# Moving GpSimd's two-input operations to VectorE in the mixers, norms and output projections of a two-layer hybrid kernel

## The chip, the cores and the metric

The kernel runs on one core of a Trainium2 chip. The metric is device time of one execution in microseconds (us); lower is better. The engines are named as in the profile: PE is TensorE (PEld its weight loads), DVE is VectorE, ACT is ScalarE, POOL is GpSimd, SP is SyncE, which issues nearly all DMAs.

## What is computed

Two layers act on 640 tokens (128 of a context pass, 512 of a denoising step) of 1024 channels. Each layer is a normalised four-way mixer followed by a convolutional FFN, both with residuals:

```python
h = rmsnorm(x, norm1_w) * (1 + sc1) + sh1
pa, pb, pc, pd = split(h @ w_in)            # SSD, retention, S5, RG-LRU
y = concat([ssd(pa), ret(pb), s5(pc), lru(pd)]) @ w_out
x = x + g1 * y
h = rmsnorm(x, norm2_w) * (1 + sc2) + sh2
g, u = split(h @ w_up)
x = x + g2 * ((silu(dwconv(g)) * u) @ w_down)
```

The six vectors sh, sc, g come from a modulation matrix product of the conditioning vector. After the second layer there is one more rmsnorm. The final states of the four scans are outputs too.

## The kernel before

**Layout and precision.** Activations are held channels by tokens: eight tiles of 128 x 640, worked in two halves of 320 columns. The second half (`HALF[1]`) is done first everywhere (`HO = (1, 0)`). The first half holds the 128 context tokens and 192 of the others, which have different modulation, so a scaled operation needs two instructions there (128 and 192 columns, `CSEG`) and one of 320 in the second half.

**Three products for one.** A float32 product is made of three fp32r products (`mm3`): every operand is split into `hi` (rounded) and `lo = x - hi`. For weights this is done in `wsplit` (line 186): a DMA brings 128 x 512 floats into a ring of five `raw` buffers, ACT casts `hi`, and a TENSOR_TENSOR subtracts to make `lo`, after which the `raw` buffer is free. `lo` reads two SBUF operands. Which engine makes it alternates by a list:

```python
lo_eng = [G, V]
...
(le or lo_eng[lo_i[0] % len(lo_eng)]).tensor_tensor(lo, raw, hi, op=subtract)
```

`G` is GpSimd, `V` is VectorE. The first two weight tiles of a projection (`first_tiles`, line 232) ask for `G` by `le`.

**The norm** (`Norm`, line 358). `add` squares each of the eight tiles on ACT (`nsq`) and sums them (`nacc`), the sum alternating between G and V; a matmul with ones sums over channels; `rsqrt_of` makes `nrs` on DVE. `apply` then does for each k: `nt = x * am * nrs` (DVE), `hhi = nt + sh` (ACT), and `hlo`: for even k one DVE SCALAR_TENSOR_TENSOR per segment, for odd k `nt + sh` on ACT and then one subtraction on G.

**The mixers.** `s5_mixer` runs eight blocks, each a chain of matmul, four DVE operations, two scans (`s5r`), and the turn back, in which G makes two of four operations. `lru_mixer` ends in a product `ylru` on G. `ssd_mixer` works in five chunks for two head pairs; in each, `sE` goes ACT, DVE, ACT, G, DVE. `ret_mixer` rotates four tiles (`rq`, one product on G) and scales queries (`qe`, G). The output projection has two parts (tiles `w_o1`, `w_o2`), each fed by `wsplit`; the second norm's `add` and `apply` run between its matmuls.

**Order.** Every engine takes its instructions in program order. The program order is made when the kernel is built, by a scheduler that lays out a timeline from its own costs; the code only gives priorities and a few fixed orders. So an edit of which engine does what can shift the order on all engines. All work is recorded through one helper, and every row of the profile therefore says L92: tiles tell the operations apart.

**The FFN** (`layer`, from `f = 0`) uses the same `wsplit`. Its loops run over 22 tiles of up-projection in groups of 6, 6, 6 and 4, with a part of the down-projection after each.

Of the kernel before, what the change touches and what calls it, by code (L numbers as in the profile page):

```python
# [13 lines left out]
ALU = mybir.AluOpType  # L14
# [13 lines left out]
CSEG = (((0, 128, 1), (128, 192, 0)), ((0, 320, 0),))  # L28
# [47 lines left out]
def hybrid_kernel(ctx: ExitStack, tc: tile.TileContext, I, O, dbg=None):  # L76
# [33 lines left out]
    V, G, A, T, SP = Eng(nc.vector), Eng(nc.gpsimd), Eng(nc.scalar), Eng(nc.tensor), Eng(nc.sync)  # L110
# [33 lines left out]
    def r2f(ap):  # L144
        return ap.bitcast(F32)
# [37 lines left out]
    lo_eng = [G, V]  # L183
# [48 lines left out]
    def first_tiles(units, act, steps=None):  # L232


        ws = [wsplit(u, 1024, le=G) for u in units]
        out = [[None, None] for _ in ws]
        for ks in steps or ():
            for h in HO:
                for i, (w, o) in enumerate(zip(ws, out)):
                    if o[h] is None:  # L240
                        o[h] = bank("a" if i and h == HO[1] else "mm")
                    col_tile(w, act, halves=(h,), ks=ks, out=o[h])
        if steps:
            return out
        for h in HO:
            for w, o in zip(ws, out):
                o[h], = col_tile(w, act, halves=(h,))
        return out
# [109 lines left out]
    class Norm:  # L358
# [6 lines left out]
        def add(self, k, h, tag="mod", tail=False):  # L365

            o, n = HALF[h]
            acc = self.acc[:, o:o + n]
            if k == 0:
                A.activation(acc, x[k][:, o:o + n], AF.Square, scale=1.0 / 32.0)  # L370
                return
            sq = page("Yb", name="nsq")[:, :n]
            A.activation(sq, x[k][:, o:o + n], AF.Square, scale=1.0 / 32.0)
            if k < 7 or h == HO[0]:
                (G if k in (1, 3, 5) and not tail else V).tensor_tensor(acc, acc, sq, op=ALU.add)
            if k < 7:
                return
            ps = bank(tag)[:, :n]
            T.matmul(ps, C("ones"), acc, start=True, stop=h == HO[0])
            if h == HO[1]:  # L380
                T.matmul(ps, C("ones"), sq, start=False, stop=True)
            rsqrt_of(ps, acc, sq, self.rs[:, o:o + n])
# [14 lines left out]
        def apply(self, l, i, h, hh, ks=range(8)):  # L397

            am, sh = amul[l][i], modT[l][3 * i]
            o, n = HALF[h]  # L400
            for k in ks:
                t = page("Yc" if k % 4 < 2 else "Yd", name="nt")
                hi, lo = [v[:, o:o + n] for v in hh[k]]
                for a, w, c in CSEG[h]:
                    w = slice(a, a + w)
                    V.scalar_tensor_tensor(t[:, w], x[k][:, o:o + n][:, w], am[:, k, c:c + 1], self.rs[:, o:o + n][:, w],
                                           op0=ALU.mult, op1=ALU.mult)
                for a, w, c in CSEG[h]:
                    w = slice(a, a + w)
                    A.activation(hi[:, w], t[:, w], AF.Identity, bias=sh[:, k, c:c + 1])  # L410
                for a, w, c in CSEG[h]:
                    w = slice(a, a + w)
                    if k % 2:
                        A.activation(t[:, w], t[:, w], AF.Identity, bias=sh[:, k, c:c + 1])
                    else:
                        V.scalar_tensor_tensor(lo[:, w], t[:, w], sh[:, k, c:c + 1], r2f(hi[:, w]),
                                               op0=ALU.add, op1=ALU.subtract)
                if k % 2:
                    G.tensor_tensor(lo, t[:, :n], r2f(hi), op=ALU.subtract)

    def h_pages():
        return [(page("H", F32R, "hhi"), page("H", F32R, "hlo")) for _ in range(8)]
# [69 lines left out]
    M_, A_, S_ = ALU.mult, ALU.add, ALU.subtract  # L492
# [298 lines left out]
    def s5_mixer(l, hh, y, steps):  # L791
        u = []
# [37 lines left out]
        def scans(q):  # L830

            wbt, tbt = page("B", name="wb"), page("B", name="tb")
            SP.dma_start(wbt[:, 0:512], wb[q])
            block(wbt[:, 512:640], 2 * q)
            SP.dma_start(tbt[:, 0:652], tb[q, :, 0:652])
            ps = bank("b")
            for k in range(4):
                T.matmul(ps[:, TB * k:TB * k + TB], wbt[:, 128 * k:128 * k + 128], u[q // 4][:, 2 * (q % 4) + k // 2],
                         start=True, stop=True)

            def gi(t):
                return t.rearrange("p (g i c) -> p g i c", g=2, i=2)


            pv, tv = gi(ps[:, 0:W]), gi(tbt[:, 0:W])
            cb, sb = [tv[:, :, i:i + 1, :].to_broadcast([P, 2, 2, TB]) for i in range(2)]
            wa, wr = page("B", name="s5a"), page("B", name="s5r")
            G.memset(tbt[:, 652:653], 0.0)
            ta = gi(wa[:, 1:329])[:, :, :, 0:TB]
            t2 = gi(wa[:, 329:653])  # L850
            V.tensor_tensor(ta, pv, cb, op=M_)
            V.tensor_tensor(t2, pv[:, :, ::-1, :], sb, op=M_)
            V.tensor_tensor(ta[:, :, 0], ta[:, :, 0], t2[:, :, 0], op=A_)
            V.tensor_tensor(ta[:, :, 1], ta[:, :, 1], t2[:, :, 1], op=S_)
            G.memset(wa[:, 0:1], 0.0)
            G.tensor_copy(wa[:, 1:329].rearrange("p (g i c) -> p g i c", g=2, i=2)[:, :, :, 16:82:65],
                          s5x0[l][:, 2 * q:2 * q + 2])
            d0, d1 = DH
            V.tensor_tensor_scan(wr[d0, 1:329], tbt[d0, W:W + 328], wa[d0, 0:328], 0.0, op0=M_, op1=A_)
            V.tensor_tensor_scan(wr[d1, 0:328][:, ::-1], tbt[d1, W + 1:W + 329][:, ::-1], wa[d1, 1:329][:, ::-1], 0.0,  # L860
                                 op0=M_, op1=A_)

            rv, xa = gi(wr[:, 0:328]), gi(wr[:, 329:653])
            r_ = gi(wr[:, 1:329])[:, :, :, 0:TB]
            V.tensor_tensor(xa, r_, cb, op=M_)
            G.tensor_tensor(t2, r_[:, :, ::-1, :], sb, op=M_)
            V.tensor_tensor(xa[:, :, 0], xa[:, :, 0], t2[:, :, 0], op=S_)
            G.tensor_tensor(xa[:, :, 1], xa[:, :, 1], t2[:, :, 1], op=A_)

            for d, c in enumerate((17, 0)):  # L870
                A.copy(fin[DH[d], :, 2 * q:2 * q + 2].rearrange("p i g -> p g i"), rv[DH[d], :, :, c])
            return wbt, xa
# [51 lines left out]
        for i in range(2):  # L924
            tp = page("B", name="glut")
            for h in range(2):
                o, n = HALF[h]
                t = tp[:, o:o + n]
# [12 lines left out]
    def lru_mixer(l, hh, y):  # L941
# [13 lines left out]
        n = 644  # L955
        hs = []
# [54 lines left out]
        yield  # L1011
        for i in range(2):
            for a, w, s in ((0, 128, P0), (128, 512, S0)):
                G.tensor_tensor(y[i][:, a:a + w], y[i][:, a:a + w], hs[i][:, s:s + w], op=M_)

    def gates(l, hh, units, out, func):

# [53 lines left out]
    def ssd_mixer(l, hh, y):  # L1071
# [98 lines left out]
        for t in range(2):  # L1170
# [3 lines left out]
            tokens(xt, chunk_cols, "c", lambda ps, k0, n: A.copy(xk[:, k0:k0 + n], ps))  # L1174
            xs = [paged("C", [5, 128], "sxs") for _ in range(2)]
            for d in range(2):
                G.tensor_tensor(xs[d].rearrange("p k (g c) -> p k g c", g=2), xk.rearrange("p k (g c) -> p k g c", g=2),
                                tw[:, d, t].unsqueeze(3).to_broadcast([P, 5, 2, 64]), op=M_)
            S = enter_states("C", "c", I["st_ssd"][l], t, btok, xs, lambda d, k: cd[:, k, d, t:t + 1], so[:, :, t])
            gtag = "a" if t else "c"  # L1180
            for k in range(5):
# [7 lines left out]
                for g in range(2):  # L1189
                    h = 2 * g + t  # L1190
# [7 lines left out]
                if k:  # L1198
# [2 lines left out]
                        rows = slice(64 * g, 64 * g + 64)  # L1201
                        A.activation(ce[rows], cb[rows, 0:512].rearrange("p (d g c) -> p d g c", d=2, g=2)[:, :, g, :], AF.Exp)
                    V.tensor_tensor(ce, ce, cr[:, c0:c0 + 128].unsqueeze(1).to_broadcast([P, 2, 128]), op=M_)
                G.tensor_tensor(e, e, dm, op=M_)
                for g in range(2):
                    hs = slice(128 * g, 128 * g + 128)
                    V.tensor_tensor(dm[:, hs], e[:, hs], gp[g][:, k], op=M_)
# [30 lines left out]
    def ret_mixer(l, hh, y):  # L1238
# [9 lines left out]
        def rotated(u):  # L1248
            pss = col_tile(wsplit(I["w_in"][l, u], 1024), hh)
            q = page("A", name="rq")  # L1250
            evac(pss, q)
            sw = page("A", name="rsw")
            V.stream_shuffle(sw[:, :512], q[:, 128:640], swap)
            V.tensor_tensor(sw[:, :512], sw[:, :512], sinp[:, :512], op=M_)
            G.tensor_tensor(q[:, 128:640], q[:, 128:640], cosp[:, :512], op=M_)
            V.tensor_tensor(q[:, 128:640], q[:, 128:640], sw[:, :512], op=A_)
            return q

        def attend(t, q, kx):
# [7 lines left out]
            S = enter_states("A", "b", I["st_ret"][l], t, ktok, vs, lambda d, k: rcd[:, d, t:t + 1], so[:, :, t])  # L1267
            qe = [paged("A", [4, 128], "qe") for _ in range(2)]
            for d in range(2):
                G.tensor_tensor(qe[d], q[:, 128:640].rearrange("p (k c) -> p k c", c=128),  # L1270
                                rrow[:, d, t, :].unsqueeze(1).to_broadcast([P, 4, 128]), op=M_)
            m = [paged("A", [5, 128], "rM") for _ in range(2)]
            for k0, n in ((0, 4), (4, 1)):
# [85 lines left out]

    def layer(l, norm):  # L1360
        sec[0] = f"norm{l}"
        hh = h_pages()
        steps = [range(2 * q, 2 * q + 2) for q in range(4)] if l == 0 else None
        for ks in steps or (range(8),):
# [66 lines left out]
        for h in HO:  # L1431
# [5 lines left out]
                norm.add(m, h)  # L1437
            norm.apply(l, 1, h, h2)
        f = 0
        if l + 1 < L:  # L1440
            mod_queue(l, (5,), "B")
            mod_queue(l + 1, range(6), "B")
# [301 lines left out]
```

## Time and profile before

| what | value |
|---|---|
| median of 3 runs | 1761.01 us (1759.26 to 1765.38) |
| the profiled execution | 1760.15 us, its span 1758.3 us |
| busy in the span | PE 1659.0, PEld 1532.9, DVE 1042.9, ACT 712.0, POOL 466.2 us |
| granted TensorE clock, mean of the span | 0.971 |
| chain that ended last | PE 77%, DVE 10%, DMA 4%, ACT 3%, POOL 2% |

By the trace, layer 0 has its start and mixers from 0 to about 400 us, its second norm around 400 to 450, its FFN to about 900; layer 1 has its first norm from about 940 to 975, mixers to 1245, second norm to 1310, FFN to 1740; the rest is the final norm. A row of a group gives operation, tiles, shapes and count, then busy us and mean ns, then the idle time of the engine before it. A granted clock of 1.00 is the 2.4 GHz level of TensorE; a lower mean says what share of the stretch was at 1.2 GHz.

### The profile page before, as it was taken

The numbers are of one execution on the slowest core, as the hardware profiler recorded it, in microseconds if no ns is written. First come the engines' busy times: TensorE is split into PE (matmuls) and PEld (weight loads), VectorE is DVE, ScalarE is ACT, GpSimd is POOL, SyncE is SP. The second block draws the span as 40 slices with busy tenths as digits, with TensorE's granted clock in tenths as the row PEclk, the third lists the DMA queues.
The fourth block names the chain that finished last, engine by engine and source line by source line (L and its number), as shares of the span: only waits on it lengthen the run. The fifth ranks groups of instructions, "written<-read, shape, count | busy, mean of one in ns | idle before, by whom it ended". The sixth has DMA issues, their size and how long they took to land.

```text
span 1758.3 us, 30749 instructions
## 1 busy us (share of the span) xinstructions
PE 1659.0 (94%) x11342; PEld 1532.9 (87%) x11342; DVE 1042.9 (59%) x2482; ACT 712.0 (40%) x1566; POOL 466.2 (27%) x652
## 2 busy tenths in 40 slices
PE   7877999999999999999988999899999999999997
PEld 3655787888999999999988889798889999999996
DVE  7776976977433773455367678588753343334345
ACT  5724534645321343332335364555453233233244
POOL 2221343413211211221223244432332111211222
PEclk9977999999999999999999999999999999999998
DMA  9465564321435445543333334422112222222321
GB/s 323 148 203 144 176 204 135 90 75 49 125 124 164 152 159 182 184 144 114 97 94 129 113 103 135 144 76 75 37 60 61 79 84 64 88 76 60 94 73 61
DMA packets 143433, 206.50 MB, mean 117 GB/s; under 512 B 22852, under 2 KB 64692, under 8 KB 143284
## 3 DMA queue, kind: packets, MB, share of 16 engines
q1 hardware_dynamic: 143284, 204.54, 37.3%
q8 instruction: 90, 1.47, 0.3%
q14 instruction: 59, 0.48, 0.1%
HBM read 184.42 MB, written 20.07 MB: 116 GB/s over the span
## 4 chain that ended last, share of the span: by engine, by line
PE 77%; DVE 10%; DMA 4%; ACT 3%; issue 3%; POOL 2%; SPq 0%; DVEq 0%; POOLq 0%; ACTq 0%
PE mm L92 65%; PE b L92 6%; PE mod L92 4%; PE c L92 2%; DMA mraw<-in_mod_w 1%; DVE nt L92 1%; DVE x L92 1%; DVE s5r L92 1%; PE a L92 1%; DVE lo L92 1%; POOL lo L92 1%; DVE nsq L92 1%; DMA wb<-wb 1%; ACT hhi L92 1%; DVE sE L92 1%
## 5 line engine op out<-in xcount | busy, mean ns | idle before, releaser
L92 PE MATMUL mm<-hhi,hi 128*128 128x320 f32 x1976 | 624.0, 317 | 17.1 <-ACT hhi L92 11.1
L92 PE MATMUL mm<-hlo,hi 128*128 128x320 f32 x1976 | 622.5, 315 | 5.5 <-POOL hlo L92 2.9
L92 PE MATMUL mm<-hhi,lo 128*128 128x320 f32 x1976 | 617.6, 314 | 0.3 <-DVE lo L92 0.3
L92 ACT CAST hi<-raw 128x512 fp32r<-128x512 f32 (+1 forms) x384 | 227.2, 593 | 594.6 <-PE mm L92 358.5
L92 POOL TENSOR_TENSOR lo<-raw,hi 128x512 fp32r<-128x512 f32 (+1 forms) x200 | 258.0, 1291 | 675.1 <-ACT hi L92 615.3
L92 PEld LDWEIGHTS mm<-hhi,hi 128*128 128x128 f32 x1976 | 375.3, 190 | 37.1 <-ACT hhi L92 16.0
L92 PEld LDWEIGHTS mm<-hlo,hi 128*128 128x128 f32 x1976 | 375.3, 190 | 15.4 <-POOL hlo L92 5.5
L92 PEld LDWEIGHTS mm<-hhi,lo 128*128 128x128 f32 x1976 | 374.9, 190 | 4.3 <-issue 2.2
L92 DVE TENSOR_TENSOR lo<-raw,hi 128x512 fp32r<-128x512 f32 (+1 forms) x184 | 127.3, 692 | 210.3 <-ACT hi L92 202.4
L92 DVE SCALAR_TENSOR_TENSOR x<-mm,mod,x 128x320 f32<-128x320 f32 (+2 forms) x288 | 117.4, 435 | 208.5 <-PE mm L92 206.9
L92 PE MATMUL mm<-fal,hi 128*128 128x320 f32 x640 | 197.4, 309 | 0.0
L92 PE MATMUL mm<-fah,lo 128*128 128x320 f32 x640 | 197.3, 309 | 0.0
L92 PE MATMUL mm<-fah,hi 128*128 128x320 f32 x640 | 195.2, 311 | 0.2 <-DVE x L92 0.2
L92 PEld LDWEIGHTS mm<-fah,hi 128*128 128x128 f32 x640 | 119.2, 188 | 5.4 <-issue 2.5
L92 PEld LDWEIGHTS mm<-fah,lo 128*128 128x128 f32 x640 | 120.4, 188 | 0.4 <-issue 0.4
L92 PEld LDWEIGHTS mm<-fal,hi 128*128 128x128 f32 x640 | 120.4, 188 | 0.0
L92 DVE TENSOR_TENSOR fa<-fc,mm 128x128 f32<-128x128 f32 x132 | 45.2, 373 | 98.1 <-PE mm L92 92.5
L92 PE MATMUL mod<-mraw,s 128*32 128x256 f32 x768 | 69.2, 415 | 18.7 <-DMA mraw<-in_mod_w 18.1
L92 DVE SCALAR_TENSOR_TENSOR fc<-fraw,par,fc 128x643 f32<-128x643 f32 x88 | 81.1, 923 | 2.8
L92 PE MATMUL mm<-yhi,hi 128*128 128x320 f32 x192 | 60.6, 317 | 1.6 <-DVE rg L92 1.1
L92 PE MATMUL mm<-ylo,hi 128*128 128x320 f32 x192 | 60.8, 317 | 1.2 <-DVE ylo L92 1.2
L92 PE MATMUL mm<-yhi,lo 128*128 128x320 f32 x192 | 61.1, 318 | 0.0
(350 smaller groups left out, 2425.7 us busy)
## 6 DMA issues: line engine op xcount, KB each, us to landing
raw<-in_up SPq DMA_DIRECT2D x176, 256.0 KB
mraw<-in_mod_w SPq DMA_DIRECT2D x160, 256.0 KB
raw<-in_w_in SPq DMA_DIRECT2D x80, 256.0 KB
raw<-in_dn SPq DMA_DIRECT2D x96, 192.0 KB
mraw<-in_mod SPq DMA_DIRECT2D x32, 256.0 KB
raw<-in_w_o SPq DMA_DIRECT2D x32, 256.0 KB
tb<-tb SPq DMA_DIRECT2D x16, 326.0 KB
x<-in_x SPq DMA_DIRECT2D x16, 320.0 KB
```

The lines of the kernel that those rows point to most:

```text
L92: r = f(*a, **k)
```

## The change

Every operation of GpSimd with two SBUF inputs goes to VectorE, except those of the FFN and the last scaling of the output. The list `lo_eng` is set to `[V]` at the start of a layer and back to `[G, V]` where its FFN begins. In `apply`, odd k in the second half becomes one DVE operation instead of one on ACT and one on G; in the first half G's subtraction goes to V. The diff, with unchanged lines left out:

```diff
@@ first_tiles
-        ws = [wsplit(u, 1024, le=G) for u in units]
+        ws = [wsplit(u, 1024, le=V) for u in units]
@@ Norm.add
-                (G if k in (1, 3, 5) and not tail else V).tensor_tensor(acc, acc, sq, op=ALU.add)
+                V.tensor_tensor(acc, acc, sq, op=ALU.add)
@@ Norm.apply
-                    if k % 2:
+                    if k % 2 and len(CSEG[h]) > 1:
                         A.activation(t[:, w], t[:, w], AF.Identity, bias=sh[:, k, c:c + 1])
                     else:
                         V.scalar_tensor_tensor(lo[:, w], t[:, w], sh[:, k, c:c + 1], r2f(hi[:, w]),
                                                op0=ALU.add, op1=ALU.subtract)
-                if k % 2:
-                    G.tensor_tensor(lo, t[:, :n], r2f(hi), op=ALU.subtract)
+                if k % 2 and len(CSEG[h]) > 1:
+                    V.tensor_tensor(lo, t[:, :n], r2f(hi), op=ALU.subtract)
@@ s5_mixer, scans
-            G.tensor_tensor(t2, r_[:, :, ::-1, :], sb, op=M_)
+            V.tensor_tensor(t2, r_[:, :, ::-1, :], sb, op=M_)
...
-            G.tensor_tensor(xa[:, :, 1], xa[:, :, 1], t2[:, :, 1], op=A_)
+            V.tensor_tensor(xa[:, :, 1], xa[:, :, 1], t2[:, :, 1], op=A_)
@@ lru_mixer
-                G.tensor_tensor(y[i][:, a:a + w], y[i][:, a:a + w], hs[i][:, s:s + w], op=M_)
+                V.tensor_tensor(y[i][:, a:a + w], y[i][:, a:a + w], hs[i][:, s:s + w], op=M_)
@@ ssd_mixer
-                G.tensor_tensor(xs[d].rearrange("p k (g c) -> p k g c", g=2), xk.rearrange("p k (g c) -> p k g c", g=2),
+                V.tensor_tensor(xs[d].rearrange("p k (g c) -> p k g c", g=2), xk.rearrange("p k (g c) -> p k g c", g=2),
...
-                G.tensor_tensor(e, e, dm, op=M_)
+                V.tensor_tensor(e, e, dm, op=M_)
@@ ret_mixer
-            G.tensor_tensor(q[:, 128:640], q[:, 128:640], cosp[:, :512], op=M_)
+            V.tensor_tensor(q[:, 128:640], q[:, 128:640], cosp[:, :512], op=M_)
...
-                G.tensor_tensor(qe[d], q[:, 128:640].rearrange("p (k c) -> p k c", c=128),
+                V.tensor_tensor(qe[d], q[:, 128:640].rearrange("p (k c) -> p k c", c=128),
@@ layer
         sec[0] = f"norm{l}"
+        lo_eng[:] = [V]
...
         f = 0
+        lo_eng[:] = [G, V]
```

In the built programs 205 instructions leave POOL and 205 come to DVE, and 16 leave ACT; PE, ACT and DVE otherwise have the same instructions, and SP issues the same number. The 205 are 64 `lo`, 32 `hlo`, 21 `nacc`, 20 `sE`, 16 `s5a`, 16 `s5r`, 8 each of `qe`, `rq`, `sxs` and `ylru`, and 4 `wlo`. Of the 64 `lo`, 32 lie before the end of the second norm of layer 0, 32 between there and the second norm of layer 1. Three places show what moved.

POOL, layer 1, where the first half of the LRU mixer ends (`lst` its final state, `s5a<-s5x` the entry state of the next S5 block). Before:

```order
L92 TENSOR_TENSOR lo<-raw,hi 128x512
L92 COPY lst<-lg 128x1 x2
L92 TENSOR_TENSOR lo<-raw,hi 128x512
L92 COPY s5a<-s5x_1_111 128x4x2
L92 TENSOR_TENSOR ylru<-ylru,lg 128x128
L92 TENSOR_TENSOR ylru<-ylru,lg 128x512
L92 TENSOR_TENSOR s5a<-s5r,tb 128x324
L92 TENSOR_TENSOR s5r<-s5r,s5a 128x2x81
```

The same place of POOL with the change:

```order
L92 COPY s5a<-s5x_1_111 128x4x2
L92 COPY lst<-lg 128x1 x2
L92 MEMSET tb 128x1
L92 MEMSET s5a 128x1
L92 COPY s5a<-s5x_1_111 128x4x2
```

The copy of the entry state no longer stands behind a `lo`. On DVE the two scans of that S5 block (64x328, written as SCALAR_TENSOR_TENSOR) and the gate `yssd`, which empties a PSUM bank for the next projection, stood like this before:

```order
L92 TENSOR_TENSOR lg<-lg 128x644
L92 SCALAR_TENSOR_TENSOR s5r<-tb,s5a 64x328 x2
L92 SCALAR_TENSOR_TENSOR yssd<-yssd,mm 128x320
L92 TENSOR_TENSOR s5r<-s5r,tb 128x324
L92 TENSOR_TENSOR s5r<-s5r,s5a 128x2x81
```

With the change:

```order
L92 SCALAR_TENSOR_TENSOR s5r<-tb,s5a 64x328 x2
L92 SCALAR_TENSOR_TENSOR lxc<-lraw,par_76,lxc 128x643
L92 TENSOR_TENSOR lg<-lg 128x644
L92 TENSOR_TENSOR lo<-raw,hi 128x512
L92 TENSOR_TENSOR s5r<-s5r,tb 128x324
L92 TENSOR_TENSOR s5a<-s5r,tb 128x324
L92 SCALAR_TENSOR_TENSOR yssd<-yssd,mm 128x320
L92 TENSOR_TENSOR ylru<-ylru,lg 128x128
```

Five operations now stand between the scans and `yssd`, where there was none.

DVE, layer 1, second norm, its last half of columns (the first in memory), where the norm's output is handed to the FFN; a tile's number tells one tile from the next. Before:

```order
L92 SCALAR_TENSOR_TENSOR hlo_14045<-nt_14432,mod1_3_95,hhi_14044 128x128
L92 SCALAR_TENSOR_TENSOR hlo_14045<-nt_14432,mod1_3_95,hhi_14044 128x192
L92 SCALAR_TENSOR_TENSOR hlo_14049<-nt_14447,mod1_3_95,hhi_14048 128x128
L92 SCALAR_TENSOR_TENSOR hlo_14049<-nt_14447,mod1_3_95,hhi_14048 128x192
L92 SCALAR_TENSOR_TENSOR nt_14462<-x_13722,am1_1_101,nrs_14043 128x128
```

With the change:

```order
L92 SCALAR_TENSOR_TENSOR hlo_14033<-nt_14416,mod1_3_95,hhi_14032 128x128
L92 SCALAR_TENSOR_TENSOR hlo_14033<-nt_14416,mod1_3_95,hhi_14032 128x192
L92 SCALAR_TENSOR_TENSOR hlo_14037<-nt_14431,mod1_3_95,hhi_14036 128x128
L92 TENSOR_TENSOR hlo_14035<-nt_14423,hhi_14034 128x320
L92 SCALAR_TENSOR_TENSOR nt_14446<-x_13710,am1_1_101,nrs_14031 128x128
L92 SCALAR_TENSOR_TENSOR hlo_14037<-nt_14431,mod1_3_95,hhi_14036 128x192
```

The subtraction of the first odd tile (14035), POOL's before, now stands behind the first even tile and one short operation of the next.

## Rows read from the trace of the kernel before

**Rows 1.** The page, part 1: busy us and share of the span.

```profile
PE 1659.0 (94%) x11342; PEld 1532.9 (87%) x11342; DVE 1042.9 (59%) x2482; ACT 712.0 (40%) x1566; POOL 466.2 (27%) x652
```

**Rows 2.** Windows by stage: length, busy us of PE, PEld, DVE, ACT, POOL, clock, DMA.

```profile
160.00:400.00 240.00, 227.82 (x1572) 200.85 (x1571) 192.43 (x427) 115.88 (x269) 84.41 (x117) 0.99 0.43 131
900.00:975.00 75.00, 64.80 (x398) 60.96 (x397) 48.56 (x96) 37.56 (x87) 28.47 (x28) 0.91 0.37 113
975.00:1245.00 270.00, 255.53 (x1730) 233.83 (x1728) 206.65 (x446) 137.27 (x307) 97.74 (x140) 0.99 0.34 105
1245.00:1310.00 65.00, 59.58 (x367) 56.19 (x366) 44.86 (x89) 33.24 (x74) 24.60 (x33) 0.95 0.14 45
1310.00:1720.00 410.00, 410.00 (x2794) 410.00 (x2794) 153.71 (x277) 121.43 (x233) 82.70 (x120) 1.00 0.25 75
```

**Rows 3.** Windows, one stretch where DVE is densest.

```profile
1000.00:1040.00 40.00, 38.85 (x262) 36.65 (x261) 37.79 (x78) 24.11 (x46) 14.98 (x34) 1.00 0.38 113
```

**Rows 4.** Groups by shape, POOL, whole span.

```profile
L92 POOL TENSOR_TENSOR lo<-raw,hi 128x512 fp32r<-128x512 f32 x152 | 208.5, 1373 | 461.1 <-ACT hi L92 407.4 <-DMA wc<-pmi 17.2 <-PE mm L92 14.0
```

**Rows 5.** Groups by shape, DVE, the FFN of layer 1 alone (1320 to 1720).

```profile
L92 DVE TENSOR_TENSOR lo<-raw,hi 128x512 fp32r<-128x512 f32 x38 | 26.2, 691 | 86.0 <-ACT hi L92 85.2
L92 DVE TENSOR_TENSOR fal<-fa,fah 128x640 fp32r<-128x640 f32 x20 | 16.5, 826 | 2.9 <-ACT fah L92 2.5
L92 DVE SCALAR_TENSOR_TENSOR x<-mm,mod,x 128x320 f32<-128x320 f32 x24 | 13.2, 550 | 24.0 <-PE mm L92 24.0
L92 DVE TENSOR_TENSOR fa<-fc,mm 128x320 f32<-128x320 f32 x20 | 9.8, 488 | 22.8 <-PE mm L92 22.8
L92 DVE SCALAR_TENSOR_TENSOR x<-mm,mod,x 128x128 f32<-128x128 f32 x24 | 8.4, 351 | 58.4 <-PE mm L92 58.4
```

**Rows 6.** Groups by shape, DVE, whole span.

```profile
L92 DVE SCALAR_TENSOR_TENSOR nt<-x,am,nrs 128x320 f32<-128x320 f32 x32 | 23.4, 765 | 0.1
L92 DVE SCALAR_TENSOR_TENSOR sE<-ct,dt,sE 128x128 f32<-128x128 f32 x40 | 21.0, 549 | 5.1 <-ACT sE L92 4.8
```

**Rows 7.** Groups by shape, DVE, the mixers of layer 1 (975 to 1245).

```profile
L92 DVE TENSOR_TENSOR lo<-raw,hi 128x512 fp32r<-128x512 f32 x22 | 17.9, 813 | 7.4 <-DMA wb<-zz 5.1 <-ACT hi L92 1.2 <-PE mm L92 1.1
```

**Rows 8.** Timeline of POOL, 1180 to 1192: start, us, engine, operation.

```profile
1183.21 1.55 POOL L92 TENSOR_TENSOR lo<-raw,hi 128x512 fp32r<-128x512 f32 x1 [0.82 <-ACT hi L92]
1188.53 3.04 POOL L92 TENSOR_TENSOR qe<-rq,ct 128x512 f32<-128x512 f32 x2
```

**Rows 9.** Timeline of DVE, 1180 to 1192.

```profile
1183.53 1.38 DVE L92 SCALAR_TENSOR_TENSOR sE<-scb,cum,sE 128x128 f32<-128x128 f32 x1
1188.63 1.78 DVE L92 TENSOR_TENSOR lo<-raw,hi 128x512 fp32r<-128x512 f32 x1
```

**Rows 10.** Waits of PE, 160 to 400: total us, times, longest.

```profile
PE mm L92 <- DVE ylo L92: 1.2, 1, 1.2
```

**Rows 11.** Waits of PE, 900 to 975.

```profile
PE mm L92 <- POOL hlo L92: 1.3, 1, 1.3
```

**Rows 12.** Waits of PE, 975 to 1245.

```profile
PE mm L92 <- ACT yhi L92: 2.7, 1, 2.7
PE mm L92 <- DVE yssd L92: 1.8, 1, 1.8
PE mm L92 <- DVE rg L92: 1.1, 1, 1.1
```

**Rows 13.** Waits of PE, 1245 to 1310.

```profile
PE mm L92 <- POOL hlo L92: 1.0, 1, 1.0
```

**Rows 14.** Chain that ended last, 336 to 347: start, us, what.

```profile
338.90 1.70 DVE ylo L92
```

**Rows 15.** Chain that ended last, 1222 to 1244.

```profile
1235.33 1.82 DVE ylo L92
```

**Rows 16.** Timeline of POOL, 1030 to 1046.

```profile
1037.83 3.15 POOL L92 TENSOR_TENSOR lo<-raw,hi 128x512 fp32r<-128x512 f32 x1
```

**Rows 17.** Waits of POOL, 975 to 1245.

```profile
POOL lo L92 <- ACT hi L92: 66.4, 18, 13.0
```

## The prediction

> **What bounds the kernel now.** I read the page first, then the busy times of each engine by stage, then what PE waits for in each stage, and last the groups of POOL and DVE by shape. PE is busy for 94% of the span [rows 1]. In the second layer's FFN it is busy in every microsecond at a granted clock of 1.00 [rows 2]: there nothing on another engine can change the time, and the change leaves that part alone. What can change is what PE loses between the FFNs: 12.2 us in the first layer's mixers (240 less 227.8), 10.2 around the second layer's first norm, 14.5 in its mixers, 5.4 around its second norm [rows 2]. The start before 160 us waits for transfers and for its own chain; I count it as unchanged.
>
> So the gain is bounded by some 42 us of PE's idle time plus what the clock falls by after a stall, not by the engines' load. The reader should see next that PE's waits have many causes, and that only a few end at POOL or at a DVE operation that POOL held up [rows 10 to 13].
>
> **Why POOL slows DVE.** At 1183.21 POOL starts a `lo` of 1.55 us. DVE's `sE` of 128 x 128, which starts 0.3 us later, takes 1.38 us [rows 8, 9]; an operation of that shape takes 0.35 where nothing stands beside it [rows 5]. At 1188.63 DVE's own `lo` takes 1.78 beside two `qe` on POOL [rows 8, 9], where the FFN's take 0.69 [rows 5]. Each such meeting costs DVE about 1.0 to 1.1 us. The same shows in means: `nt` of 320 columns takes 0.765 and `sE` 0.549 over the span [rows 6], against 0.550 and 0.351 for scalar-tensor operations of these widths in the FFN, which read PSUM too [rows 5].
>
> **What the change moves.** 205 instructions come to DVE. 64 `lo` at 0.691 make 44.2 us; 16 `hlo` in scalar-tensor form at 0.550 make 8.8; 53 of about 320 columns (16 `hlo`, 21 `nacc`, 16 `s5a`) at 0.488 make 25.9; 36 of 256 and 162 columns (`sE`, `s5r`) lie between 0.351 and 0.488, at 0.42 they make 15.1; the other 36, mostly 512 wide, at 0.691 make 24.9 [rows 5]. Together 119 us. POOL needed about twice that: its `lo` takes 1.373 [rows 4].
>
> Against this stands what DVE gets back. At least: 32 `nt` by 0.215, 40 `sE` by 0.198 and 22 `lo` of the second layer's mixers by 0.122 (0.813 against 0.691), which is 17.5 us [rows 5 to 7]. At most: all 119. I take one meeting of 1.05 us for every third of the 205, 70 us, because the two meetings above are ordinary ones and the three groups are only a part of DVE's two-input operations. So DVE's load rises by about 49 us (0 to 102), over stretches in which it is idle for 47.6, 26.4, 63.4 and 20.1 us [rows 2], 157 in all. On the whole it fits. ACT loses 16 activations of `nt`; no wait of PE ends there, so I count nothing. No DMA is added; the `raw` ring is now freed by DVE in place of POOL.
>
> **The sum on PE's path.** Five places:
> - First layer, `ylo` before the output projection: PE waits 1.2 us [rows 10]; the chain holds a `ylo` of 1.70 [rows 14] that takes 0.83 undisturbed (the 640-wide subtraction of rows 5). I take 0.9 of it (0 to 1.2).
> - `hlo` on POOL in the second layer's two norms: PE waits 1.3 and 1.0 us [rows 11, 13]. With the change DVE does it behind one short operation. I take all 2.3 (0 to 2.3).
> - `yssd`: PE waits 1.8 us [rows 12]; a POOL `lo` of 3.15 [rows 16] held up the entry state that the scans wait for. It goes, but five operations now stand between the scans and `yssd`, by rows 5 about 0.6 us each, 3.0 together. I take 0 (a gain of 1.8 to a loss of 1.5).
> - `rg`: PE waits 1.1 us [rows 12], behind the DVE `lo` of 1.78 of rows 9, which goes to 0.69: 1.1 (0 to 1.1).
> - `yhi` of the last mixer: PE waits 2.7 us [rows 12], behind a `ylo` of 1.82 [rows 15] that goes to 0.83: 1.0 (0 to 1.0).
>
> That is 5.3 us. Against it: in each of the three norms inside the layers, DVE has nine more operations between the two halves (three `lo`, four `hlo`, two `nacc`, counted in the built program of the last one; 2.1 + 2.2 + 1.0 = 5.3 us). It is full there already, and what follows is late by what is not given back. `nt` alone gives back 1.7 of it on the means (8 by 0.215); I take 4.8 in all, since POOL works beside nearly every operation of that stretch, and so a loss of 0.5 a norm, 1.5 (0 to 3.5 a norm). The clock: its mean of 0.91 over 75 us and 0.95 over 65 [rows 2] are 13.5 and 6.5 us at the 1.2 GHz level, 6.8 and 3.3 of full-speed work lost, at stages where PE first stands still and then goes on at the lower level. Fewer stops may keep the level; I take a third, 3.4 (0 to 10). The shorter chains of S5 and SSD end at no wait of PE that I can name: 0 (a gain or a loss of 5).
>
> The sum is 5.3 - 1.5 + 3.4 = 7.2 us. From the profiled execution, 1760.15, that gives 1752.9; the median of the runs stands 0.9 above that execution, so **1754**.
>
> **The rivals.**
> *More comes back.* The clock does not fall in the norms at all, and the first layer's second norm, the same code, gains the mean of these two, 5.0: 5.3 + 10.1 + 5.0 - 1.5 = 18.9 us: 1742. For it: nearly every DVE group with two SBUF inputs is stretched. Against it: most of PE's waits of rows 2 have other causes than those in the sum.
>
> *Nothing comes back.* Each wait that goes uncovers the next: after `hlo` the cast of the tile on ACT, after `ylo` the norm of retention that feeds it. Then the five gains shrink to what the norms lose: 1761, give or take 4. For it speaks that PE is 94% busy, and that only six waits are touched. Beside it: the Trainium skill, page Perfetto Trace Analysis, section Optimizing Scalar/DVE Operations, says of moving operations between VectorE and GpSimd that it "might not help", because they share a read port. Rows 8 and 9 show the sharing; by the sentence the sum would be 0.
>
> *A `lo` blocks DVE.* This one ends slower. On POOL a `lo` that waits for its cast holds up little: in the second layer's mixers it did so for 66.4 us in 18 waits [rows 17]. DVE's own 22 waited 1.2 us for ACT [rows 7]. Now 64 more stand in DVE's queue, ahead of scans, `sE` and `yssd`. If each stalled DVE for s on the mean, between 0.05 and 3.7 us by these rows, and half of that reached PE, the gain is eaten from s = 0.22 us (64 x 0.22 / 2 = 7.0). At 0.6 the loss is 19 less 7: 1773. Against it: the order is made with `lo` on DVE known, and DVE's `lo` hardly wait today.
>
> *DVE fills up.* From 1000 to 1040 us DVE is busy for 37.8 of 40 us, POOL for 15.0 [rows 3]. At half of POOL's price (0.691 against 1.373) that is 7.5 us on 2.2 idle; if nothing came back, 5.3 too much there, and with one such stretch in either layer 1771. It decides only if less than 5.3 of the 7.5 comes back there. Beside it: the same page and section holds that where VectorE is saturated, work may well be given to ScalarE or even GpSimd, which is the reverse of this change; by that rule the time would be this one. Rows 8 and 9, where DVE waits for POOL, speak against it.
>
> That the change does not do what it says is excluded: the built program has the 205 on DVE.
>
> **How the numbers follow.** Forecast 0.35 (its own range 1749 to 1758), more 0.18, nothing 0.25, blocking 0.17, filling 0.05. About 0.3% is what a measurement can tell from no change, 5.3 us: below 1755.7 is faster, above 1766.3 slower. Faster: three quarters of the forecast, all of "more", a little of "nothing": 0.26 + 0.18 + 0.04 = 0.48. Slower: nearly all of the last two: 0.21. Same: 0.31. The range 1739 to 1769 holds the forecast, "nothing", three quarters of "more" and the milder part of the slower cases.
>
> **What would show it.** Right, if in the new trace `nt` of 320 columns has a mean near 0.55 and `sE` near 0.35, DVE's busy time is up by about 50 us, POOL's is near 230, the waits of PE for POOL's `hlo` and for `rg` are gone and the FFN of the second layer lasts as long as before. Wrong, if DVE's waits for ACT's cast grow by tens of us in the mixers, if the norms' stretches are longer than before, or if the gain sits before 160 us, which I left out.

## The result and the profile after

The changed kernel takes 1735.76 us (median of 4 runs, 1731.61 to 1739.01) against 1761.07 beside it: a ratio of 0.9852, 95% interval 0.9824 to 0.9879, or 26 us less with 21 and 31 as bounds. The forecast was 1754 with a range down to 1739: the sign was right, the gain more than three times as large. The profiled execution took 1739.01 (span 1737.2), the slowest of its four.

Part 1 of the page after (answers to [rows 1]), and by engine the chain that ended last:

```profile
PE 1650.5 (95%) x11342; PEld 1535.1 (88%) x11342; DVE 1051.8 (61%) x2687; ACT 704.6 (41%) x1550; POOL 228.6 (13%) x447
...
PE 75%; DVE 7%; DMA 2%; ACT 1%; issue 1%; POOL 0%; SPq 0%; DVEq 0%; POOLq 0%; ACTq 0%
```

In this profile the chain can be followed back to 234 us only: its shares add up to 86% and do not compare with those of before. POOL lost 237.6 us; DVE, with 205 operations more, gained only 8.9. PE's busy time fell by 8.5 for the same matmuls, its idle time by 12.6. Windows by stage, first of the kernel before, then after: the start (until PE takes the first product of the RG-LRU's gates, `a<-lxc`), the first layer's mixers (until the next norm's first `nrs`), the second layer's mixers (from one norm's second `nrs` to the next norm's first); columns as in [rows 2].

```profile
0.00:117.00 117.00, 88.03 (x540) 60.95 (x541) 86.51 (x378) 62.98 (x159) 23.37 (x39) 0.87 0.69 231
117.00:413.00 296.00, 270.53 (x1857) 230.86 (x1856) 225.57 (x488) 135.43 (x310) 94.42 (x133) 0.95 0.43 131
958.81:1259.94 301.13, 282.33 (x1887) 259.39 (x1886) 223.95 (x489) 152.83 (x349) 107.33 (x148) 0.98 0.31 96
```

```profile
0.00:112.00 112.00, 88.06 (x542) 62.64 (x543) 83.57 (x395) 60.49 (x153) 3.29 (x21) 0.88 0.72 240
112.00:403.00 291.00, 268.94 (x1857) 232.74 (x1856) 226.85 (x557) 137.49 (x312) 16.89 (x65) 0.95 0.43 134
953.38:1239.37 285.99, 277.52 (x1883) 257.30 (x1884) 229.75 (x566) 150.45 (x348) 18.04 (x67) 0.98 0.33 101
```

The start gives 5 us, the first mixers 5, the second layer's mixers 15. The three norms together take 4 back (0.9, 2.4 and 0.9, from first to second `nrs`), and the FFNs stay within 1.4. Of the 15 us, 10.3 are idle time of PE (18.8 to 8.5).

DVE's groups after (answer to [rows 5 to 7]), then three of before that were not shown:

```profile
L92 DVE TENSOR_TENSOR lo<-raw,hi 128x512 fp32r<-128x512 f32 x200 | 138.9, 696 | 182.6 <-ACT hi L92 167.8 <-DMA raw<-in_up 6.7 <-DMA raw<-in_dn 4.0
L92 DVE TENSOR_TENSOR_SCAN s5r<-tb,s5a 64x328 f32<-64x328 f32 x32 | 26.7, 835 | 2.3 <-POOL s5a L92 0.9 <-POOL tb L92 0.3 <-POOL sraw L92 0.3
L92 DVE SCALAR_TENSOR_TENSOR sxc<-sraw,par,sxc 128x643 f32<-128x643 f32 x24 | 21.2, 885 | 2.8 <-ACT sxc L92 2.5
L92 DVE SCALAR_TENSOR_TENSOR nt<-x,am,nrs 128x320 f32<-128x320 f32 x32 | 16.4, 546 | 0.1
L92 DVE SCALAR_TENSOR_TENSOR sE<-ct,dt,sE 128x128 f32<-128x128 f32 x40 | 13.4, 358 | 0.1
L92 DVE TENSOR_TENSOR_SCAN lg<-lg,lT 128x644 f32<-128x644 f32 x8 | 12.0, 1495 | 0.1
```

```profile
L92 DVE TENSOR_TENSOR_SCAN s5r<-tb,s5a 64x328 f32<-64x328 f32 x32 | 30.6, 955 | 4.6 <-POOL s5a L92 2.8 <-POOL lT L92 0.9
L92 DVE SCALAR_TENSOR_TENSOR sxc<-sraw,par,sxc 128x643 f32<-128x643 f32 x24 | 27.1, 1129 | 1.2 <-ACT sxc L92 0.9
L92 DVE TENSOR_TENSOR_SCAN lg<-lg,lT 128x644 f32<-128x644 f32 x8 | 14.4, 1800 | 0.0
```

The operations that did not move got shorter too: `nt` 0.765 to 0.546, `sE` 0.549 to 0.358, the convolution `sxc` 1.129 to 0.885, both scans by an eighth to a sixth. All of these but `nt`, which is the norms', are links of the mixers' chains. Part of such a chain before, from the view of the chain that ended last (start, us, what), in the second layer's mixers:

```profile
1077.06 1.85 POOL ylru L92 x2
1078.91 1.70 POOL rq L92
...
1081.64 1.29 POOL lo L92
...
1084.58 1.14 POOL s5a L92
...
1085.99 1.03 DVE lo L92
...
1087.54 3.46 DMA wc<-wc
...
1111.34 1.63 DVE lo L92
```

PE's waits in these mixers (total us, times, longest), first three of before that [rows 12] left out, then the four longest after:

```profile
PE b L92 <- ACT ktok L92: 4.0, 1, 4.0
...
PE b L92 <- DMA wc<-wc: 1.9, 2, 1.3
...
PE a L92 <- DVE lxc L92: 1.1, 1, 1.1
```

```profile
PE mm L92 <- ACT yhi L92: 2.6, 1, 2.6
PE mm L92 <- ACT hhi L92: 1.8, 1, 1.8
PE mm L92 <- DVE hlo L92: 1.1, 1, 1.1
PE b L92 <- DMA wc<-wc: 0.8, 1, 0.8
```

The waits for `ktok` (retention's keys, which ACT copies out of PSUM), `lxc` (the RG-LRU's convolution), `yssd` and `rg` are gone, though the first ended at ACT, not at POOL or DVE. `yhi` is where it was.

### The profile page after: what moved, and what is told of

Its sections match the earlier page's. It is cut to its first block, busy times and chain, and to the rows that moved or that the text cites. A ratio compares the mean times of both kernels' runs of the same rounds, so it can differ in the third digit from the quotient of the medians.

```text
span 1737.2 us, 30635 instructions
## 1 busy us (share of the span) xinstructions
PE 1650.5 (95%) x11342; PEld 1535.1 (88%) x11342; DVE 1051.8 (61%) x2687; ACT 704.6 (41%) x1550; POOL 228.6 (13%) x447
## 4 chain that ended last, share of the span: by engine, by line
PE 75%; DVE 7%; DMA 2%; ACT 1%; issue 1%; POOL 0%; SPq 0%; DVEq 0%; POOLq 0%; ACTq 0%
PE mm L92 64%; PE b L92 6%; PE mod L92 3%; PE c L92 2%; DVE x L92 1%; DVE nt L92 1%; DVE lo L92 1%; PE a L92 1%; DMA raw<-in_dn 1%; DVE hlo L92 1%; DVE nacc L92 0%; DVE nsq L92 0%; DVE S L92 0%; DMA wb<-wb 0%; DMA mraw<-in_mod_w 0%
## 5 line engine op out<-in xcount | busy, mean ns | idle before, releaser
L92 DVE TENSOR_TENSOR lo<-raw,hi 128x512 fp32r<-128x512 f32 (+1 forms) x248 | 166.2, 671 | 213.1 <-ACT hi L92 198.3
L92 POOL TENSOR_TENSOR lo<-raw,hi 128x512 fp32r<-128x512 f32 (+1 forms) x136 | 165.5, 1217 | 530.3 <-ACT hi L92 514.1
L92 POOL MEMSET fraw<- 128x2 f32 x132 | 9.0, 102 | 410.1 <-DVE nrs L92 210.5
L92 PEld LDWEIGHTS mod<-mraw,s 128*32 128x32 f32 x768 | 21.2, 112 | 44.7 <-issue 23.4
```

Of the source, the lines that this page charges most:

```text
L92: r = f(*a, **k)
```

## The experiments

Three theories. **Contention**: while POOL reads SBUF, DVE's operations with two inputs there stand still, and the mixers' chains run through them. **Latency**: POOL's operations are slow themselves, and their results come late. **Order**: the scheduler, told of other engines, puts the instructions in a better order. The ratio is to the kernel before, run beside it on the same chip.

| run | what | median us | ratio to before (95%) |
|---|---|---|---|
| e1_lo | before, only `lo` moved | 1746.73 | 0.9912 (0.9894 to 0.9930) |
| e2_norm | before, only the norms' part | 1765.46 | 1.0009 (0.9998 to 1.0020) |
| e3_mix | before, only the mixers' operations | 1753.26 | 0.9946 (0.9930 to 0.9961) |
| e4_lomix | e1 and e3 together | 1742.48 | 0.9887 (0.9869 to 0.9904) |
| e10_lo_norm | e1 and e2 together | 1759.03 | 0.9976 (0.9962 to 0.9990) |
| e12_changed | the changed kernel | 1734.51 | 0.9836 (0.9821 to 0.9850) |
| e5_read2 | changed, POOL reads two inputs | 1770.40 | 1.0050 (1.0032 to 1.0068) |
| e7_read1 | changed, POOL reads one input | 1745.14 | 0.9910 (0.9891 to 0.9928) |
| e6_memset | changed, POOL only writes | 1738.56 | 0.9865 (0.9848 to 0.9883) |
| e9_late | changed, `lo` late from POOL | 1737.85 | 0.9858 (0.9842 to 0.9875) |
| e8_ffnlo | changed, FFN's `lo` on DVE too | 1732.54 | 0.9829 (0.9810 to 0.9849) |
| e11_best | e8, `ys` and copies on ACT | 1738.51 | 0.9855 (0.9839 to 0.9871) |

### Parts of the change

e1 takes from the diff the two lines on `lo_eng` and `le=V`; e2 those of `add` and `apply`; e3 the seven lines in the mixers.

> Only the 64 `lo` of the weights move from POOL to DVE; norms and mixers' elementwise operations stay on POOL. Contention theory (DVE's two-input operations stand still while POOL works beside them): `lo` are 88 of the 238 us that leave POOL, so the gain is about 88/238 of the 25.3 us, 9 us (1752), and DVE's means fall only in part (`nt` of 320 columns between 0.55 and 0.77, `sE` between 0.35 and 0.55). Latency theory (what counts is that POOL's own operations are slow and their results late for the next engine): no `lo` of a weight ended a wait of PE in the mixers, so at most 3 us (1758).

> Only the norms' operations move (21 `nacc`, 32 `hlo` in one form or the other). Contention theory: 53 operations of some 1.0 us on POOL, 53/238 of the gain would be 5 us, but DVE is full in these stretches and the halves of each norm came 0.9 to 2.5 us further apart in the changed kernel: between a gain of 3 and a loss of 3 (1758 to 1764). Latency theory: PE waits no more for POOL's `hlo`, but as long for DVE's: 1761.

> Only the mixers' own operations move (16 in S5, `ylru`, `sxs`, 20 `sE`, `rq`, `qe`). Contention theory: they are about 90 us of POOL, 90/238 of the gain, 10 us (1751); `sE`, `nt` and `lo` on DVE stay stretched where POOL's `lo` stand beside them. Latency theory: nearly the whole gain, since these are the operations that stand in the mixers' chains: 20 us or more (1741).

> All of the change but the norms' part. If the norms' part costs what their longer halves show (0.9, 2.5 and 0.9 us), this is 4 us faster than the whole change: 1731. If the norms' part gains by freeing DVE from POOL (contention), it is 3 to 5 us slower than the whole change: 1740. If lo and the mixers' part simply add up, it stands as far below the kernel before as the first and third run together.

`lo` alone brings 15.5 us (0.0088 of 1762), the mixers' operations 9.5, both 19.9, the norms' part nothing. That speaks against latency, which put nearly all on the mixers' operations, though contention by POOL's load alone (9 and 10 us) misses `lo` as well. In e1 `sxc` falls to 0.962, `nt` only to 0.715; in e3 `nt` stays at 0.765, as contention has it. e4 is not faster than the whole: the norms' part costs nothing on top of it. Why it should bring 6 there was open, so e10 was run:

> The `lo` and the norms' part together, the mixers' operations left on POOL. The norms' part alone cost 1.6 us, on top of the other two it brought 6.2 (both uncertain by some 2 to 5 us). If it pays only once POOL's `lo` have left the norms' stretches (each of its operations then runs undisturbed on DVE): 15.5 + 6 less than before, 1740. If the parts simply add up: 15.5 - 1.6, 1747.

Both numbers missed: with the norms' part, `lo` brings only 4. The loss is not in the norms: the second layer's mixers last 287.3 us, as after, but the first layer's, whose operations stand on the same engines as in e1, went from 295 to 310. There the clock shows 0.91 (e1 0.95; the window of e10), and PE has a wait that before and e1 do not have in this stretch (PE's waits in e10):

```profile
109.00:420.00 311.00, 281.26 (x1863) 240.13 (x1864) 228.40 (x519) 137.16 (x312) 59.42 (x107) 0.91 0.40 126
```

```profile
PE c L92 <- ACT sso L92: 5.4, 2, 3.6
```

From e1 to e10 the built order differs from 32 us on, over the start and the first mixers. So another order can go with some 15 us in that stage, of which 11 are PE's busy time at the lower clock (269.2 us in e1, 280.4 in e10), and partial changes do not add up. What order itself gives the change there stays open: no run held the order and put the work back on POOL.

### Work that nobody waits for

These add to the changed kernel. Up to the second layer's mixers DVE's order in them is the changed kernel's (e12), row by row, and PE's but for a few rows in the first layer's mixers; from the second layer's mixers on their orders differ. Up to the first layer's second norm e5 and e6 have the same order on PE, DVE and ACT.

```
+            cast = A.copy(hi[:, :w], raw[:, :w])
...
+            if (le is not None or len(lo_eng) == 1) and lo_i[0] % 2 == 0:
+                for d in dummies(w):
+                    tc.add_manual_dep(d.ins, cast.ins.name, ...)
...
+    def dummies(w):   # e5; e7: tensor_scalar on ct, twice; e6: memset, four times
+        return [G.tensor_tensor(scr, ct[:, :256], ct[:, 256:512], op=ALU.subtract) for _ in range(2)]
```

> The changed kernel with work added that nobody waits for: at every place where a `lo` went from POOL to DVE, POOL does two subtractions of 256 columns on constants in SBUF (two inputs, result thrown away), released by the same cast. Contention theory: DVE's two-input operations stand still beside them again, so about what moving `lo` gained comes back, 10 to 16 us (1746 to 1752), and the means of `sxc` (0.885), `nt` of 320 columns (0.546) and `sE` (0.346) rise by a good tenth or more. Latency theory: no engine takes a result from these operations; only what stands behind them in POOL's queue is later: at most 4 us (1740).

> The same as the run before, but POOL writes a constant to the scratch tile four times in place of the two subtractions, so that it is as busy as long, and reads nothing. Contention by reading: no change against the changed kernel (1736, within 4), means of DVE as there. If POOL's being busy is what costs (its queue), or its writing, the same loss as with the subtractions.

> The same again, with POOL multiplying one constant tile by a number: one input in SBUF in place of two. If reading with two inputs is what blocks DVE: as with the writes, no change (1736). If any reading blocks it: as with two inputs, 10 us or more. In between, about half (1742).

Against the changed kernel (mean ratio 0.9844) the two inputs cost 36 us, one input 12, the writes 4 at most (the intervals touch). There were 60 such places. The page's busy times of e5 and, by groups, its added operations and `sxc`; then the same two views of e6:

```profile
PE 1668.9 (94%) x11342; PEld 1545.2 (87%) x11342; DVE 1088.1 (62%) x2687; ACT 707.3 (40%) x1551; POOL 345.9 (20%) x567
```

```profile
L92 POOL TENSOR_TENSOR scr<-ct 128x256 f32<-128x256 f32 x120 | 117.4, 979 | 392.9 <-ACT hi L92 357.0 <-ACT whi L92 17.0 <-issue 11.0
...
L92 DVE SCALAR_TENSOR_TENSOR sxc<-sraw,par,sxc 128x643 f32<-128x643 f32 x24 | 22.3, 928 | 2.2 <-ACT sxc L92 2.1
```

```profile
PE 1647.6 (95%) x11342; PEld 1528.0 (88%) x11342; DVE 1051.6 (61%) x2687; ACT 705.8 (41%) x1550; POOL 300.7 (17%) x687
```

```profile
L92 POOL MEMSET scr<- 128x256 f32 x240 | 75.0, 313 | 399.0 <-ACT hi L92 368.6 <-ACT whi L92 19.0 <-ACT s5fin L92 1.5
...
L92 DVE SCALAR_TENSOR_TENSOR sxc<-sraw,par,sxc 128x643 f32<-128x643 f32 x24 | 21.2, 883 | 2.0 <-ACT sxc L92 1.7
```

With the same 2687 operations DVE is busy 36.3 us longer in e5 (0.31 for each of POOL's 117.4), 10.1 longer in e7 (0.08 for each of 126.6), and no longer in e6. The start and the first mixers together, in e5 and then in e6:

```profile
0.00:415.24 415.24, 362.90 (x2397) 297.52 (x2398) 330.53 (x951) 197.89 (x465) 76.47 (x142) 0.92 0.50 159
0.00:397.93 397.93, 351.37 (x2397) 288.85 (x2398) 310.49 (x951) 198.27 (x465) 54.81 (x198) 0.95 0.52 166
```

In the same order DVE is busy 20.0 us longer and the stretch lasts 17.3 longer; the changed kernel needs 403.1 there and, in e12, 397.2, the kernel before 413.2. So POOL's reading slows DVE and through it the kernel; its being busy does not, as far as e6 goes (its writes fill 75 us, e5's subtractions 117). Two sizes were missed. The means of `sxc`, `nt` and `sE` in e5 rise by 3 to 8%, not by a tenth, and e5 costs 36 us (some 17 of them with the order held), not 10 to 16, more than twice what moving `lo` brought. POOL works longer in it than the 64 `lo` did (92 us: 208.5 of [rows 4] less the FFN's 116.2), and DVE has the `lo` besides; that these two make the rest is argued, not shown.

### A late result without reading

```
+                for c in (0, 256, 0, 256):
+                    m = G.memset(r2f(lo[:, c:c + 256] ...), 0.0)
+                    tc.add_manual_dep(m.ins, cast.ins.name, ...)
```

> The changed kernel, but every second `lo` of the mixers, norms and output projections is on POOL again, as four writes of a constant in place of the subtraction (the weights' low halves are left out there, so the output is not the reference's). So the result comes from POOL about as late as before the change (4 x 0.31 us by the writes of the earlier run, 1.37 for the subtraction), but POOL reads nothing. Latency theory: what moving `lo` gained is lost again, 10 to 16 us (1746 to 1752). Contention theory: nothing is lost, and DVE has 40 us less to do: 1736 or up to 8 us faster.

The writes stand in place of the subtraction. PE now takes 56 of the `lo` from POOL again, and nothing of the gain is lost but 2.5 us or less (0.9858 against 0.9844). That speaks against latency, for `lo`; it does not settle it, since e9's order differs from 32 us on, and the `raw` buffer is free here after the cast, not after the subtraction. The run says a second thing: DVE is busy for 1017.4 us, 34.4 less, and the kernel is not faster. In the second layer's mixers:

| kernel | length us | DVE busy | POOL busy |
|---|---|---|---|
| before | 301.1 | 224.0 | 107.3 |
| e2_norm | 304.0 | 228.7 | 100.3 |
| e5_read2 | 298.8 | 242.0 | 70.0 |
| e7_read1 | 293.6 | 233.5 | 71.9 |
| e3_mix | 293.1 | 230.8 | 62.6 |
| e1_lo | 288.9 | 227.8 | 69.5 |
| e4_lomix | 287.6 | 228.0 | 26.9 |
| after, e12 | 286.0, 283.3 | 229.8, 229.5 | 18.0, 18.6 |
| e9_late | 285.5 | 215.7 | 46.3 |
| e6_memset | 284.2 | 229.7 | 49.0 |

Neither column orders the lengths. DVE has 8 us less to do in e9 than before and the stage is 16 shorter; POOL is as busy in e1 as in e5. Both kernels whose added POOL work reads nothing are fast, in different orders of instructions. With POOL equally busy, e1 and e5 differ by 10 us, so its microseconds alone do not set the length. The reading that fits is that a `lo` on DVE runs where DVE would be idle, while a `lo` on POOL stretches whatever DVE does beside it, the links of a chain too; in this stage, where the orders differ, that is argued, not shown.

### The FFN, and a faster version

```
         f = 0
-        lo_eng[:] = [G, V]
+        lo_eng[:] = [V]
```

> The changed kernel with the FFN's `lo` on DVE too, so that none is left on POOL. Contention theory: POOL's `lo` stretch DVE in the FFN as well (POOL's take 1.22 there, DVE's means are stretched), but PE is busy in every microsecond there: no change (1736, within 4), save where the FFN's last `lo` stand beside the second norms. A theory by which DVE's whole load counts would see a loss: the FFNs get 136 more operations of 0.69, 94 us.

> The version without any `lo` on POOL, and with `ys` and the small copies (`s5a`, `lst`, `lT`) on ACT in place of POOL: some 25 us of POOL's reading of SBUF go, and `ys` takes 0.4 on ACT against 1.16. Contention theory: one-input operations of POOL cost DVE 0.08 us for each of theirs, 2 us here, of which a part reaches the time; the LRU's chain gets shorter by its copies, 1 us a scan: 1729 (1726 to 1733). Rival: ACT, whose casts release DVE's `lo`, is held up by the copies: 1736.

> The changed kernel itself, unaltered, beside the three others on the same chip, as their baseline: 1736.

e8 takes POOL's busy time down to 57.8 us; its ratio and that of e12 lie within each other's interval: in the FFNs, where PE hardly stops, taking POOL's `lo` away brings nothing that shows. e11 is 4 us above e12 (0.9855 against 0.9836), not 5 below: ACT's copies bring nothing. That ACT's casts are held up was the rival; it stays open. No version was shown to beat the changed kernel.

## Why the prediction was wrong

**The bound** was right: the second layer's FFN lasts 460.2 us against 461.6, and the gain lies outside the FFNs.

**Why POOL slows DVE** was right and is now shown (e5, e6). The FFN's prices, read as undisturbed though POOL is busy there too (82.7 of 410 us, [rows 2]), hold: DVE's `lo` takes 0.688 in e8, `sE` 0.346 in e6. The size of the refund was the first term mis-sized: "one meeting of 1.05 us for every third of the 205, 70 us". DVE rose by 8.9 us, so about 110 of the 119 came back. That refund is no gain by itself, as e9's 34 us show.

**The sum's failing step** is "The shorter chains of S5 and SSD end at no wait of PE that I can name: 0". In the second layer's mixers 10.3 us of PE's idle time went. Among the waits that went are 6.9 us that the sum did not name: `ktok` on ACT (4.0), `lxc` (1.1), the load of `wc` (1.9, of which 0.8 stay) and `ys` (0.7). The sum counted waits by the engine at their end and took POOL and DVE alone as touched. For the load of `wc` the chain quoted above shows what was missed: it runs through `ylru`, `rq`, `lo` and `s5a` on POOL and a `lo` on DVE before it comes to that load.

The largest, `ktok`, went another way. ACT before:

```profile
1140.95 0.69 ACT L92 ACTIVATE sE<-scb,ncum 128x128 f32<-128x128 f32 x2 [1.07 <-DMA scb<-cumd]
1141.55 0.82 ACT L92 ACTIVATE scb<-scb 64x256 f32<-64x256 f32 x2
1142.39 0.59 ACT L92 COPY ktok<-b 128x512 f32<-128x512 f32 x1
```

The copy stood behind operations that waited for a transfer of `scb`; with the change they no longer stand before it. The wait is gone in e1 too, which leaves the mixers' operations on POOL, and e9, where POOL adds no reading, has 2.2 us of it. So the gain of these mixers holds both less contention and a better order, and how the 15 us divide stays open; contention with the order held is shown for the stretch before (17.3 us, e5 against e6).

The chain's share does not divide them either. Of that stage 67% of the chain was PE (`mm`, `b`, `c`, `a`, `mod`) before and 85% after, but in e2, where the stage lasts 304.0 us, it is 79%, and in e1, at 288.9, 68%. Before, after and e2:

```profile
by line: PE mm L92 43.1%; PE b L92 16.4%; issue 6.8%; PE c L92 3.6%; POOL lo L92 2.4%; PE a L92 2.2%; DVE lo L92 2.1%; DVE sE L92 1.9%; DVE s5r L92 1.8%; DMA scb<-cumd 1.5%; DVE ylo L92 1.5%; PE mod L92 1.5%; DVE S L92 1.2%; DMA wc<-wc 1.1%
```

```profile
by line: PE mm L92 54.3%; PE b L92 20.5%; PE c L92 5.8%; PE a L92 3.0%; DMA wb<-wb 1.9%; issue 1.6%; PE mod L92 1.5%; DMA tb<-tb 1.3%; DVE lg L92 1.0%; DVE nt L92 0.9%; DVE lT L92 0.8%; DVE rsq L92 0.7%; DVE lo L92 0.7%; DVE lxc L92 0.6%; D
```

```profile
by line: PE mm L92 52.0%; PE b L92 18.4%; PE c L92 4.9%; issue 4.0%; PE a L92 2.6%; DVE ylo L92 1.6%; DMA scb<-cumd 1.5%; PE mod L92 1.4%; DMA wc<-wc 1.3%; DVE s5r L92 1.3%; DVE sE L92 1.2%; DVE lo L92 1.2%; DVE nt L92 0.8%; DVE lxc L92 0.8
```

**The five places.** `ylo` (taken 0.9) and `rg` (1.1) went as said, `yssd` went too (taken 0, 1.8 was to be had). `yhi` stayed (2.7, now 2.6; taken 1.0). `hlo` was wrong in sign: POOL's 1.3 and 1.0 are gone, but PE's waits for DVE's `hlo` rose by 5.3, a loss of 3.0 in place of a gain of 2.3. After, around the second layer's first and second norm, each against 1.0 before:

```profile
PE mm L92 <- DVE hlo L92: 3.4, 2, 2.3
...
PE mm L92 <- DVE hlo L92: 3.9, 3, 2.3
```

**The norms** lose, as forecast, but not by what the forecast said. The two `nrs` of a norm start 17.3 to 17.4 us apart before, 18.3, 19.8 and 18.3 in the profile after and 18.2 in all three of e12: 0.9 a norm or more, against 0.5. The forecast let DVE, full there, be late by what is not given back. Between the two `nrs` of the second layer's first norm, before and in e12:

```profile
941.48:958.81 17.33, 16.08 (x100) 14.53 (x99) 16.68 (x30) 10.74 (x23) 10.55 (x9) 1.00 0.52 174
928.58:946.82 18.24, 15.78 (x102) 14.78 (x100) 16.21 (x38) 9.52 (x21) 0.00 (x0) 1.00 0.47 165
```

DVE was full, but with eight operations more it is busy 0.5 us less: all came back. What costs is PE's wait of 2.3 us for an `hlo`, and DVE then waits 2.0 us for the norm's sum, which stands behind it on PE. The Trainium skill (Perfetto Trace Analysis, Optimizing Scalar/DVE Operations) holds that where DVE is saturated, giving work to GpSimd may make sense; e2, which moves the norms' part alone and gains nothing, agrees. The Trainium skill's other sentence there, that a move between the two engines might not help because they share a port, holds as to the sharing [rows 8 and 9] and not as to the result: 26 us came.

**The clock** was sized at 3.4; PE's busy time fell by 8.5 in the profiled run and by 14.2 in e12, for the same matmuls. So this term was mis-sized too. From e6 to e5, in the stretch shown above, 11.5 of the 17.3 us are PE's busy time, at a mean granted clock of 0.92 against 0.95.

**The start** was counted "as unchanged". It gave 5 us in one profile and 8 in the other (109.3 us in e12). It is also the stage where single profiles differ most, by the clock, and e9's start lasts 117.1 in another order of instructions. Contention can cost as much: in the same order e5's start lasts 116.0 and e6's 108.5. How the gain divides stays open.

**The signs.** Two of the prediction's own signs of being wrong came: the norms' stretches are longer, and part of the gain sits before 160 us. Of its signs of being right, DVE's busy time missed: up by 8.9, not by about 50.

**The rivals.** "More comes back" had the direction and, at 1742, was nearest. "Nothing comes back" and "DVE fills up" fail by the time. "A `lo` blocks DVE" is refuted; DVE's 46 `lo` in the mixers, 967 to 1225, waited 2.6 us for their casts in all, 0.06 each, against the 0.22 that would have eaten the gain:

```profile
DVE lo L92 <- ACT hi L92: 2.6, 4, 1.2
```

## What to carry to other kernels

Price an operation on POOL that reads SBUF not by its own time but by what DVE does beside it: where DVE's chains feed PE, taking it away can be worth more than the waits that end at POOL. Before counting PE's waits by the engine at their end, follow the chain behind each: a wait for ACT or a DMA can be the end of a slow chain through POOL and DVE, as for `wc` here, or a matter of order, as for `ktok`. And when parts of a change are tried alone, see whether the scheduler's order stayed; if not, add work that nobody waits for in place of undoing a part.

## What was not expected of the hardware

POOL's kind of operation decides: per microsecond of its own time, one with two inputs in SBUF lengthened DVE's busy time by 0.31 us (e5), one with a single input by 0.08 (e7), writing a constant by nothing (e6: 1051.6 us against 1051.8). The Trainium skill (SBUF — State Buffer, SBUF: two separate sides) says that a DVE operation with two inputs there and a GpSimd operation that reads SBUF lock each other out, for the whole instruction; e6 and e5 agree that the reading decides. That page of the Trainium skill makes no difference between one and two inputs on GpSimd's side; e7 against e5 shows one, and the measurement decides. On POOL itself one input was no cheaper than two: 1.055 us for 256 columns in e7, 0.979 in e5. And 34 us less work on DVE (e9, in another order) brought no time, while 36 us of stretching (e5) cost about as much time as it lasted.
